# Layer 0's xhat scaling of the last two token blocks placed behind the MoE routing, its buffers in the late room tile

## The chip, the core and the metric

The kernel runs on one core of a Trainium2 chip: TensorE (matmuls), VectorE, ScalarE, GpSimd and SyncE, each with a queue of its own that runs in order, and 16 DMA engines. The metric is the device time of one execution in microseconds; the figure shown for a kernel is the median of its runs.

## The reference, cut to what matters

Two layers over 512 latent tokens and 256 context tokens of width 1024. Each layer is a token mixer, a residual with LayerNorm, a mixture of experts (32 experts in 4 groups, two per token), and a second residual with LayerNorm. Layer 1 handles the 512 latent tokens alone.

```python
x_lat = _layer_norm(DN_ALPHA * x_lat + m_l[2] * y_l, ln_g[layer, 0], ln_b[layer, 0])
f_l = _modulate(x_lat, m_l[3], m_l[4])
...
ffn = _hier_moe(tokens, moe_w_group[layer], moe_b_group[layer], moe_w_router[layer], moe_b_router[layer],
                moe_w1[layer], moe_w3[layer], moe_w2[layer])
x_lat = _layer_norm(DN_ALPHA * x_lat + m_l[5] * ffn[:n_lat].reshape(x_lat.shape), ln_g[layer, 1], ln_b[layer, 1])
```

Two things come out of the first LayerNorm: f, what the experts read, and the residual that is added behind them. The kernel keeps the residual in DRAM as xhat.

## The kernel before, in words

`forward` runs, for each layer, the mixer, `post_mixer`, `moe` and, after layer 0, `post_moe`. A token block is 128 tokens: T = 6 blocks in layer 0 (four latent, two context), T = 4 in layer 1.

`post_mixer` (L1290) projects the mixer's output with the weights `wo` in two column halves. In the second half it takes each block t in turn: the residual sum (L1399 to L1403), the statistics (`ln_stats`, L1266 to L1276), the logits of the router (L1351, L1352) of an earlier block, the transposes that feed them (`turn`, L1339, copied by ScalarE in L1341), and `normalise(t - 1)`. `normalise` (from L1354) does two things with a block x. ScalarE writes xh = (x - mean) / deviation (L1362). In layer 0 GpSimd multiplies xh by ALPHA times the gain `gr` (L1364) and adds ALPHA times the bias `br` (L1365), and ScalarE's queue sends xh to DRAM (`K.xhat`, L1366). Beside it VectorE turns x in place into f, in two steps (L1374, L1375), and ScalarE's queue sends f to DRAM (`K.f`, L1376). In layer 1 the last block's f is made by GpSimd out of xh (L1371, L1372), and xh goes to DRAM unscaled. xh has two buffers in layer 0, in the pool `px`; `gr`, `br` and a small `bt` for the output bias lie in `px` too.

`moe_route` (L759 to L853) then picks the experts, in some forty small VectorE operations on tiles of 128 x 24 to 128 x 192, with two ScalarE exponentials and a few matmuls. `moe_ffn` (L857) handles the experts in 16 pairs. `prep(p)` (from L1014) finds the tokens of a pair: one-hot tiles by VectorE (L875), their matmuls (L889), and an indirect DMA by GpSimd that gathers the rows of f (`load`, L902). Each `prep` leaves a function `second()` that loads the pair's larger count into a GpSimd register (L1036) and, if it is over 64 (L1037), gathers the rest. Before the loop the kernel calls `prep(0)`, `prep(1)` and the two `second()`; inside the loop over 32 experts it calls `prep(p + 2)` for every other expert and its `second()` one expert later. Experts 30 and 31 leave their rows in a tile `room`, 128 x 4096, made at expert 30 in the pool `late`.

The weights come through a ring of buffers: `Stream.pump` has SyncE issue one 2 MB load whenever a buffer is free. Two of the buffers that open behind `post_mixer` are held back on purpose, by a one-element GpSimd copy into the buffer (L190): one copy waits for the last block's f, three more stand behind the first gather.

What sets the order of the work: a planner fixes the order of each engine's queue when the kernel is compiled. It starts from the order of the source and from the dependences; `issue_after` adds such a dependence by hand. What came out is read from the trace.

Of the kernel before, what the change touches and what calls it, by code (L numbers as in the profile page):

```python
# [11 lines left out]
F = mybir.dt.float32  # L12
FR = mybir.dt.float32r
# [3 lines left out]
ALU = mybir.AluOpType  # L17
# [283 lines left out]
def row_bcast(ap, n):  # L301

    return bass.AP(tensor=ap.tensor, offset=ap.offset, ap=[[0, 128], [1, n]])
# [553 lines left out]
def moe_ffn(K, l, T, pos, val, cnt, tok0, Y, weights, pool, fx):  # L857

    nc, c = K.nc, K.cst
    V, S, G, PE = nc.vector, nc.scalar, nc.gpsimd, nc.tensor  # L860
    ps, stream = K.ps, K.stream
# [68 lines left out]
    def after(ins):  # L930
        return K.tc.issue_after(ins) if ins else nullcontext()
# [21 lines left out]
    def turn_h(h, s):  # L953
        a = 64 * s
        q = bank("q")
        for j in range(4):
            last = PE.transpose(q[:, 64 * j:64 * j + 64], h[a:a + 64, j:512:4], c["ident"][a:a + 64, a:a + 64]).ins  # L957
        hT = pool.tile([128, 4, 64], F, tag="hT", name="hT", bufs=2)
        V.tensor_copy(hT, q[:, 0:256].rearrange("p (j m) -> p j m", j=4))  # L959
        return hT, last  # L960
# [85 lines left out]
    for second in seconds:  # L1046
        second()
    seconds.clear()
    rest = nc.values_load(cnt[0:1, 64:65], min_val=0, max_val=T * 128)

    def more_blocks(w1, w3):
# [50 lines left out]
    for n in range(33):  # L1102
        p, s = divmod(n, 2)
        turned = []

        def inner():
            hT, last = turn_h(prev["h"], 1 - s)
            turned.append(hT)
            return last

        if n == ROOM:
            K.room = stream.get(("room", l)) if l else (fx.tile([128, 4096], FR, name="room"), None)
            room = K.room[0]
        if n == POST and l:
            K.posts = [stream.get(("post", l, i)) for i in range(2)]
            with after(late_ins):
                residuals(K)
        if n < 32:
            e = 2 * PAIRS[p] + s
            _, oh2, gate, idx = pairs[p]  # L1120
            slots = [stream.get((k, l, e)) for k in ("w1", "w3")]
            w1, w3 = (t[0] for t in slots)
            rv = nc.values_load(cnt[0:1, e:e + 1], engines=engs, min_val=0, max_val=T * 128)
            h = ffn_in(xT[:, :, 64 * s:64 * s + 64], w1, w3, s, gate[:, 0:1], "h", prev and inner)
            if s == 0:
                prep(p + ahead)
            elif p < 15:
                xT = turn_x(x)
        else:
            inner()  # L1130
        if prev:
            w2 = stream.get(("w2", l, prev["e"]))
            if s:
                y = pool.tile([128, 1024], F, tag="y", name="y", bufs=2)

            def second():
                with K.tc.If(prev["rv"] > 64):
                    more_out(prev["h2"], 1 - s, w2[0], prev["idx"][:, 1:2])

            q = ffn_products(turned[0], w2[0])  # L1140
            if n == 32:

                h2 = hidden("h2")
                with after(K.last_mm):
                    with K.tc.If(rv > 64):
                        second_in(15, 1)
                        more_out(h2, 1, w2[0], idx[:, 1:2])
                more_blocks(w1, w3)
                stream.done(*slots)
                sums(K, l, Y)  # L1150
            rows_out(q, y[64 - 64 * s:128 - 64 * s])
            if s == 0 and p > first_late:
                ins = rows_of(y, p - 1 - first_late)
                if n == 30:
                    late_ins = ins
            elif s == 0:
                put(y, prev["idx"][:, 0:1], slice(0, 128))
            if n < 32:
                second()
                stream.done(w2)  # L1160
            if n == 28:

                z = pool.tile([128, 512], F, tag="xTo", name="zeros")
                i2 = pool.tile([128, 4], I32, name="i2")
                G.memset(z, 0.0)
                for o in range(4 if l else 2):
                    V.tensor_scalar(i2[:, o:o + 1], pairs[first_late + o // 2][3][:, 0:1], 2.0, float(o % 2),
                                    op0=ALU.mult, op1=ALU.add)
                    put(z, i2[:, o:o + 1], slice(0, 128), 2)
        if n < 31:  # L1170
            h2 = hidden("h2")
            with K.tc.If(rv > 64):  # L1172
                second_in(p, s)
            if n == 30:
                tokens_of(pairs[15][0], 1 if l else 0)
            if n == 30 and l:
                tokens_of(slots_of(2 * PAIRS[14], 2, c["iota"], pos, "a", 1), 0)
            stream.done(*slots)
        if s == 0 and p < 15:
            x = xgs[0][(p + 1) % 2]  # L1180
        if s == 1 and seconds:
            seconds.pop()()
        if n < 32:
            prev = dict(e=e, h=h, h2=h2, rv=rv, idx=idx)
# [40 lines left out]
def row(K, pool, key, nm, bufs=1):  # L1225
    t = pool.tile([128, 1024], F, tag=nm, name=nm, bufs=bufs)
    K.nc.sync.dma_start(t, row_bcast(K.rows[key], 1024))
    return t
# [61 lines left out]
def post_mixer(K, l, T, mp, mixp, toks, extra):  # L1290

    nc, c = K.nc, K.cst
    V, S, G, PE = nc.vector, nc.scalar, nc.gpsimd, nc.tensor
    if l:
        K.xe = K.open("xearly", "left")
    px = K.open("px", "left")
    wo = K.open("wo", "right")
    cond = [0] * 4 + [1] * (T - 4)
# [3 lines left out]
    if l:  # L1302
        gb = row(K, px, ("gb", l, 0), "f10")
        ga = row(K, px, ("G1", 0), "f20")
    else:
        bo = wo.tile([33, 1024], FR, name="bo")
        bt = px.tile([128, 1024], F, tag="xh", name="bt", bufs=2)
        ones = wo.tile([33, 128], FR, name="ones")
        S.activation(ones, c["onesf"][0:33], AF.Copy)
        G.memset(bo.bitcast(F), 0.0)  # L1310
        nc.sync.dma_start(bt[0:1], K.a["ebo"])
        S.activation(bo[0:1], bt[0:1], AF.Copy)
        G.tensor_sub(bo[32:33], bt[0:1], bo[0:1].bitcast(F))
# [7 lines left out]
    with K.tc.issue_after(loaded):  # L1321
        gate = [row(K, wo, ("gate", l, i), "gate%d" % i) for i in range(nc_)]
# [1 line left out]
    fTs = {}  # L1324
    f12 = [[row(K, px, ("F%d" % n, l, 0), "f%d0" % n) for n in (1, 2)]]
    if l == 0:
        gr, br = (row(K, px, (n, l), n) for n in ("G0", "B0"))
        for r in (gr, br):
            S.activation(r, r, AF.Copy, scale=ALPHA)
    if l:  # L1330
        K.stream.add(K.xe, 3)
# [22 lines left out]
    def normalise(t):  # L1354

        x = ts[t]
        mu, rs = st[t]
        nm = px.tile([128, 1], F, tag="nm", name="nm", bufs=2)
        V.scalar_tensor_tensor(nm, mu, -1.0, rs, op0=ALU.mult, op1=ALU.mult)

        xh = gate[0] if l and t == T - 2 else px.tile([128, 1024], F, tag="xh", name="xh", bufs=2 - l)
        S.activation(xh, x, AF.Identity, scale=rs, bias=nm)  # L1362
        if l == 0:
            G.tensor_mul(xh, xh, gr)  # L1364
            G.tensor_add(xh, xh, br)  # L1365
        S.dma_start(K.xhat[l][t], xh)  # L1366
        if cond[t] == len(f12):
            f12.append([row(K, px, ("F%d" % n, l, 1), "f%d0" % n) for n in (1, 2)])
        f1, f2 = f12[-1]
        if l and t == T - 1:  # L1370
            G.tensor_mul(x, xh, f1)  # L1371
            G.tensor_add(x, x, f2)  # L1372
        else:
            V.scalar_tensor_tensor(x, x, mu, f1, op0=ALU.subtract, op1=ALU.mult)  # L1374
            V.scalar_tensor_tensor(x, x, rs, f2, op0=ALU.mult, op1=ALU.add)  # L1375
        S.dma_start(K.f[128 * t:128 * t + 128], x)  # L1376

    st = []
# [1 line left out]
    for h in range(2):  # L1380
# [8 lines left out]
        for t in range(T):  # L1389
# [8 lines left out]
            xh = ts[t][:, 512 * h:512 * h + 512]  # L1398
# [30 lines left out]
    r = moe_route(K, T, L, mo, fr)  # L1429
# [5 lines left out]
def moe(K, l, T, pools, pos, val, cnt, tok0):  # L1435

    Y = K.dram.tile([2 * T * 128, 1024], F, name="Y%d" % l)
    mo, xr = pools
    fx = None
    if l == 0:  # L1440
        fx = K.fx = K.open("late", "left")
    ff = K.open("ffn", "left")
    w = [K.a[n][l].rearrange("e (p j) f -> e p (j f)", j=j) for n, j in (("w1", 8), ("w3", 8), ("w2", 4))]
    moe_ffn(K, l, T, pos, val, cnt, tok0, Y, w, ff, fx)
    K.close(mo)
    if l:
        K.left = xr, ff, K.xe
    else:
        K.close(ff)
        K.close(xr)  # L1450
    return Y
# [129 lines left out]
def residuals(K):  # L1581

    xh, (a1, a2, _, _) = [[s[0][:, 1024 * n:1024 * n + 1024] for n in range(4)] for s in K.posts]
    V = K.nc.vector
    for x in xh:
        V.scalar_tensor_tensor(x, x, ALPHA, a1, op0=ALU.mult, op1=ALU.mult)
        V.scalar_tensor_tensor(x, a2, ALPHA, x, op0=ALU.mult, op1=ALU.add)
# [717 lines left out]
```

## Time and profile before

| | |
|---|---|
| runs | 1982.54, 1983.78 and 1989.46 us, median 1983.78 |
| the profiled execution, its own time | 1984.09 us |
| its span, first to last instruction | 1982.3 us |
| TensorE busy | 1723.8 us |
| VectorE busy | 934.8 us |
| GpSimd busy | 495.2 us |
| mean granted TensorE clock | 0.934 |

The profile is one execution; its times are counted from the span's start. Engines are PE (TensorE matmuls), PEld (its weight loads), DVE (VectorE), ACT (ScalarE), POOL (GpSimd) and SP (SyncE); a q behind a name is the engine's sequencer or its DMA queue. L1364 is line 1364 of the kernel. "xh<-xh,G" is an output and its inputs by the program's names. A row of the view in order of time has the start, the duration, the engine, the line, the operation, the tiles and shapes, how many were merged, and in brackets the idle time before it and what ended it. PEclk is the granted clock as a share of 2.4 GHz.

### The profile page before, as it was taken

How to read it: one execution, taken by the hardware profiler on the slowest of the kernel's cores; microseconds unless marked ns; L12 is line 12 of the kernel's file. 1: busy time of each engine (PE TensorE's matmuls, PEld its weight loads, DVE VectorE, ACT ScalarE, POOL GpSimd, SP SyncE). 2: the span in 40 equal slices, each digit the busy share in tenths (PEclk: the TensorE clock that was granted, in tenths of full speed). 3: DMA queues.
4: the chain of work that ended last, by engine and by line, in shares of the span. 5: the costliest groups of instructions: out<-in, count | busy, mean ns of one | idle time of the engine just before them, and what ended most of it. 6: DMA issues, size and time to landing. Idle time of an engine off the chain costs nothing. (4 is left out here: it accounts for less than half of the span.)

```text
span 1982.3 us, 22945 instructions
## 1 busy us (share of the span) xinstructions
PE 1723.8 (87%) x8347; PEld 901.1 (45%) x8355; DVE 934.8 (47%) x1651; ACT 459.0 (23%) x774; POOL 495.2 (25%) x433
## 2 busy tenths in 40 slices
PE   5989999958989999999858878999599999988795
PEld 3668556853333333333336654558433333333232
DVE  4786554782222222221187799676623223222137
ACT  3572342220100100010145453343200000000001
POOL 2153464340101000101045576443101001000103
PEclk8999999968999999999979788899799999999998
DMA  9731314258898999989961114417669999999973
GB/s 368 316 126 43 134 83 157 99 196 318 337 425 358 421 426 402 418 343 386 389 266 43 43 43 170 171 43 311 226 277 425 404 425 395 425 426 425 425 300 148
DMA packets 59022, 551.87 MB, mean 278 GB/s; under 512 B 13295, under 2 KB 13807, under 8 KB 28018
## 3 DMA queue, kind: packets, MB, share of 16 engines
q1 hardware_dynamic: 43490, 514.47, 63.5%
q0 software_dynamic: 11056, 21.00, 2.8%
q10 hardware_dynamic: 4320, 14.33, 1.9%
q8 instruction: 97, 1.59, 0.3%
q14 instruction: 59, 0.48, 0.1%
HBM read 535.02 MB, written 33.61 MB: 287 GB/s over the span
## 5 line engine op out<-in xcount | busy, mean ns | idle before, releaser
L940 PE MATMUL q<-ring,xT 128*64 128x512 f32 x1024 | 479.7, 612 | 44.5 <-PEq L1172 27.0
L941 PE MATMUL q<-ring,xT 128*64 128x512 f32 x1024 | 480.9, 614 | 6.4 <-DMA ring<-in_w_dram 3.5
L969 PE MATMUL q<-ring,hT 128*64 128x512 f32 x1152 | 300.2, 610 | 24.1 <-DMA ring<-in_w_dram 10.2
L940 PEld LDWEIGHTS q<-ring,xT 128*64 128x64 f32 x1024 | 133.4, 140 | 302.0 <-issue 269.6
L949 ACT ACTIVATE sl<-q 64x512 f32<-64x512 f32 x72 | 42.6, 591 | 756.2 <-PE q L941 745.0
L902 POOL DMA_INDIRECT xg<-f,tok x38 | 39.1, 1028 | 595.4 <-DVE tok L897 406.9
L969 PEld LDWEIGHTS q<-ring,hT 128*64 128x64 f32 x1152 | 89.2, 139 | 181.9 <-issue 168.8
L941 PEld LDWEIGHTS q<-ring,xT 128*64 128x64 f32 x1024 | 133.9, 140 | 26.0 <-issue 16.6
L959 DVE COPY hT<-q 128x256 f32<-128x256 f32 x72 | 30.6, 425 | 240.1 <-PE q L957 239.7
L278 PE MATMUL pj<-hh,wlo 128*128 128x512 f32 (+2 forms) x336 | 108.5, 373 | 15.8 <-DVE wlo L267 15.8
L278 PE MATMUL pj<-hl,whi 128*128 128x512 f32 (+2 forms) x336 | 105.9, 364 | 0.0
L278 PE MATMUL pj<-hh,whi 128*128 128x512 f32 (+2 forms) x336 | 105.3, 363 | 0.0
L1839 POOL TENSOR_TENSOR acc<-acc,prod 128x512 f32<-128x512 f32 x56 | 87.4, 1561 | 56.1 <-ACT prod L1838 53.1
L875 DVE TENSOR_TENSOR oh<-cf,pos 128x512 fp32r<-128x512 f32 (+1 forms) x65 | 53.3, 822 | 98.9 <-PE qi L889 97.9
L977 DVE TENSOR_TENSOR y<-q,m 64x512 f32<-64x512 f32 x70 | 48.2, 689 | 81.5 <-PE q L969 74.8
L980 DVE COPY y<-q 64x512 f32<-64x512 f32 x37 | 25.7, 693 | 114.4 <-ACT y L979 76.5
L915 DVE COPY xT<-qx 128x512 f32<-128x512 f32 x32 | 22.1, 692 | 120.9 <-PE qx L911 120.9
L950 DVE SCALAR_TENSOR_TENSOR h<-q,gate,sl 64x512 f32<-64x512 f32 x68 | 51.0, 749 | 56.6 <-ACT sl L949 39.2
L1834 DVE SCALAR_TENSOR_TENSOR acc<-glu,pv,acc 128x512 f32<-128x512 f32 x60 | 73.5, 1230 | 0.9
L278 PEld LDWEIGHTS pj<-hh,wlo 128*128 128x128 f32 (+1 forms) x336 | 59.1, 196 | 31.6 <-DVE wlo L267 15.9
L984 POOL DMA_INDIRECT Y<-y,idx x33 | 32.8, 993 | 147.1 <-DVEq L1172 71.7
L957 PEld LDWEIGHTS q<-cf,h 64*128 64x128 f32 x288 | 39.8, 209 | 59.3 <-issue 55.8
(530 smaller groups left out, 3087.3 us busy)
## 6 DMA issues: line engine op xcount, KB each, us to landing
ring<-in_w_dram SPq DMA_DIRECT2D x192, 2048.0 KB, 18.7
ring<-in_wmod_dram SPq DMA_DIRECT2D x24, 2048.0 KB, 10.6
ring<-Y SPq DMA_DIRECT2D x8, 1024.0 KB, 9.7
ring<-in_ew_dram SPq DMA_DIRECT2D x3, 2048.0 KB
f<-t ACTq DMA_DIRECT2D x10, 512.0 KB, 4.1
xhat<-xh ACTq DMA_DIRECT2D x9, 512.0 KB, 3.8
ring<-in_ewo_dram SPq DMA_DIRECT2D x2, 2048.0 KB, 11.0
ring<-in_ow_dram SPq DMA_DIRECT2D x2, 2048.0 KB, 16.5
```

Of the source, the lines that this page charges most:

```text
L278: nc.tensor.matmul(q[0:m, 0:s1 - s0], a[:, k, 0:m], b[k][:, s0:s1], start=(k == i == 0), stop=(k == 7 and i == 2))
L875: V.tensor_tensor(oh.rearrange("p t (n s) -> p t n s", n=n), iota[:, None, None, :].to_broadcast([128, T, n, 64]), pos[:, :, e:e + n, None ...
L902: return G.indirect_dma_start(out=x[0:m], out_offset=None, in_=K.f, in_offset=bass.IndirectOffsetOnAxis(ap=tok[0:m], axis=0), bounds_check ...
L940: PE.matmul(q[a:a + 64], xT[:, k, :], w1[:, 512 * k:512 * k + 512], start=(k == 0), stop=(k == 7))
L941: last = PE.matmul(q[b:b + 64], xT[:, k, :], w3[:, 512 * k:512 * k + 512], start=(k == 0), stop=(k == 7)).ins
L949: S.activation(sl[a:a + 64], q[a:a + 64], AF.Silu)
L950: V.scalar_tensor_tensor(h[a:a + 64], q[b:b + 64], gate[a:a + 64], sl[a:a + 64], op0=ALU.mult, op1=ALU.mult)
L957: last = PE.transpose(q[:, 64 * j:64 * j + 64], h[a:a + 64, j:512:4], c["ident"][a:a + 64, a:a + 64]).ins
L969: K.last_mm = PE.matmul(q[64 * o:64 * o + 64], hT[:, k, :], w2[:, 1024 * k + 512 * o:1024 * k + 512 * o + 512], start=(k == 0), stop=(k == ...
L977: V.tensor_mul(y[:, b], q[a], K.m5[a, b])
L1834: V.scalar_tensor_tensor(y, g[:, k:k + NL], w(k), y, op0=ALU.mult, op1=ALU.add)
L1839: G.tensor_add(z, z, p)
```

## The change

The scaling of xhat for blocks 4 and 5 of layer 0, and the DMA that stores it, become functions that `moe_ffn` calls on GpSimd behind the two `second()` ahead of the expert loop. So that xh, `gr` and `br` outlive `px`, they move into one tile `spare` in the pool `late`, which is opened before `px` and shares its room with the later `room` tile. In layer 1, the last block's f is made by VectorE as for the other blocks.

```diff
@@ moe_ffn
     seconds.clear()
+    if l == 0:
+        for scaled in K.after:
+            scaled(G)
     rest = nc.values_load(cnt[0:1, 64:65], min_val=0, max_val=T * 128)
@@
         if n == ROOM:
-            K.room = stream.get(("room", l)) if l else (fx.tile([128, 4096], FR, name="room"), None)
+            K.room = stream.get(("room", l)) if l else (fx.tile([128, 4096], FR, tag="room", name="room"), None)
@@ post_mixer
     if l:
         K.xe = K.open("xearly", "left")
+    else:
+
+        K.fx = K.open("late", "left")
+        spare = K.fx.tile([128, 4096], F, tag="room", name="spare")
+        spare = [spare[:, 1024 * n:1024 * n + 1024] for n in range(4)]
+        K.after = []
     px = K.open("px", "left")
@@
-        bt = px.tile([128, 1024], F, tag="xh", name="bt", bufs=2)
+        bt = spare[2]
@@
     if l == 0:
-        gr, br = (row(K, px, (n, l), n) for n in ("G0", "B0"))
-        for r in (gr, br):
+        gr, br = spare[0:2]
+        for r, n in ((gr, "G0"), (br, "B0")):
+            nc.sync.dma_start(r, row_bcast(K.rows[n, l], 1024))
             S.activation(r, r, AF.Copy, scale=ALPHA)
@@ normalise
-        xh = gate[0] if l and t == T - 2 else px.tile([128, 1024], F, tag="xh", name="xh", bufs=2 - l)
+        xh = spare[2 + t % 2] if l == 0 else gate[0] if t == T - 2 else px.tile([128, 1024], F, tag="xh", name="xh")
         S.activation(xh, x, AF.Identity, scale=rs, bias=nm)
-        if l == 0:
-            G.tensor_mul(xh, xh, gr)
-            G.tensor_add(xh, xh, br)
-        S.dma_start(K.xhat[l][t], xh)
+
+        def scaled(E):
+            if l == 0:
+                G.tensor_mul(xh, xh, gr)
+                G.tensor_add(xh, xh, br)
+            E.dma_start(K.xhat[l][t], xh)
+
+        if l == 0 and t > T - 3:
+            K.after.append(scaled)
+        else:
+            scaled(S)
@@
-        if l and t == T - 1:
-            G.tensor_mul(x, xh, f1)
-            G.tensor_add(x, x, f2)
-        else:
-            V.scalar_tensor_tensor(x, x, mu, f1, op0=ALU.subtract, op1=ALU.mult)
-            V.scalar_tensor_tensor(x, x, rs, f2, op0=ALU.mult, op1=ALU.add)
+        V.scalar_tensor_tensor(x, x, mu, f1, op0=ALU.subtract, op1=ALU.mult)
+        V.scalar_tensor_tensor(x, x, rs, f2, op0=ALU.mult, op1=ALU.add)
@@ moe
     if l == 0:
-        fx = K.fx = K.open("late", "left")
+        fx = K.fx
```

## Rows read from the trace of the kernel before

**Rows 1.** The page: busy time, share of the span and instructions of each engine.
```profile
PE 1723.8 (87%) x8347; PEld 901.1 (45%) x8355; DVE 934.8 (47%) x1651; ACT 459.0 (23%) x774; POOL 495.2 (25%) x433
```
**Rows 2.** Windows: us, busy PE, PEld, DVE, ACT, POOL, granted clock, DMA share, GB/s.
```profile
330.00:408.00 78.00, 78.00 (x395) 61.66 (x393) 52.70 (x91) 17.76 (x28) 27.82 (x12) 1.00 0.43 163
410.00:429.00 19.00, 8.24 (x48) 7.65 (x47) 16.23 (x31) 4.62 (x7) 11.36 (x4) 0.62 0.64 243
429.00:442.00 13.00, 3.77 (x25) 3.53 (x24) 10.26 (x50) 5.50 (x7) 0.21 (x1) 0.50 0.66 242
```
**Rows 3.** GpSimd in order of time, 411 to 430 us (layer 0, blocks 4 and 5).
```profile
412.36 2.45 POOL L1364 TENSOR_TENSOR xh<-xh,G 128x1024 f32<-128x1024 f32 x1 [3.47 <-ACT xh L1362]
414.88 3.20 POOL L1365 TENSOR_TENSOR xh<-xh,B 128x1024 f32<-128x1024 f32 x1
422.18 2.35 POOL L1364 TENSOR_TENSOR xh<-xh,G 128x1024 f32<-128x1024 f32 x1 [4.09 <-ACT xh L1362]
424.60 3.37 POOL L1365 TENSOR_TENSOR xh<-xh,B 128x1024 f32<-128x1024 f32 x1
429.19 0.21 POOL L190 COPY ring<-t 1x1 f32<-1x1 f32 x1 [1.23 <-DVE ge L772]
```
**Rows 4.** VectorE in order of time, the same stretch, logits and f steps.
```profile
413.37 2.51 DVE L1374 SCALAR_TENSOR_TENSOR t<-t,mv,f 128x1024 f32<-128x1024 f32 x1
415.81 2.33 DVE L1352 SCALAR_TENSOR_TENSOR L<-L,mv,bi 128x36 f32<-128x36 f32 x1
418.12 1.27 DVE L1375 SCALAR_TENSOR_TENSOR t<-t,mv,f 128x1024 f32<-128x1024 f32 x1
...
419.86 0.26 DVE L1352 SCALAR_TENSOR_TENSOR L<-L,mv,bi 128x36 f32<-128x36 f32 x1
...
423.27 1.30 DVE L1352 SCALAR_TENSOR_TENSOR L<-L,mv,bi 128x36 f32<-128x36 f32 x1
424.50 1.27 DVE L1374 SCALAR_TENSOR_TENSOR t<-t,mv,f 128x1024 f32<-128x1024 f32 x1
...
425.80 3.24 DVE L1375 SCALAR_TENSOR_TENSOR t<-t,mv,f 128x1024 f32<-128x1024 f32 x1
```
**Rows 5.** Lines 1036 (430 to 445 us) and 1037 (to 455): ns, first and last start.
```profile
L1036 POOLq TENSOR_LOAD <-cnt x8: 283/290/492, 439.2 to 444.6; - x8
...
L1037 POOLq COMPARE_BRANCH  x3: 38/40/55, 445.2 to 448.0; - x3
```
**Rows 6.** ScalarE in order of time: DMA issues of xhat and f.
```profile
418.33 0.33 ACTq L1366 DMA_DIRECT2D xhat<-xh  x1
...
419.42 0.85 ACTq L1376 DMA_DIRECT2D f<-t  x1
```
**Rows 7.** GpSimd in order of time, 440 to 470 us: the gathers.
```profile
442.40 1.75 POOL L902 DMA_INDIRECT xg<-f,first  x1 [12.99 <-PE qi L889]
...
466.00 0.99 POOL L902 DMA_INDIRECT xg<-f,tok  x1 [14.40 <-DVE tok L897]
```
**Rows 8.** VectorE and GpSimd in order of time, layer 1's routing.
```profile
1411.96 0.19 DVE L773 TENSOR_TENSOR ae<-ae,cf 128x32 f32<-128x32 f32 x1
...
1412.11 2.34 POOL L1371 TENSOR_TENSOR t<-xh,f 128x1024 f32<-128x1024 f32 x1 [41.25 <-ACT xh L1362]
...
1412.41 2.09 DVE L777 TENSOR_TENSOR ao<-ae,ai 128x32 f32<-128x32 f32 x1
1414.53 2.40 POOL L1372 TENSOR_TENSOR t<-t,f 128x1024 f32<-128x1024 f32 x1
...
1414.64 2.43 DVE L799 TENSOR_TENSOR A<-go,ao 128x128 f32<-128x128 f32 x1
...
1418.21 0.28 DVE L799 TENSOR_TENSOR A<-go,bo 128x128 f32<-128x128 f32 x1
```
**Rows 9.** VectorE and TensorE in order of time: h of the first expert.
```profile
462.21 0.75 DVE L950 SCALAR_TENSOR_TENSOR h<-q,gate,sl 64x512 f32<-64x512 f32 x1
...
467.80 0.45 PE L957 MATMUL q<-cf,h 64*128 64x64 f32 x2
```

## The prediction

> **What bounds the kernel now.** I read the page first, then stretches, then engines in order of time. TensorE is busy for 87% of the span [rows 1], so work of GpSimd can only count where TensorE stands still. The view by windows finds that place [rows 2]. From 330 to 408 us TensorE is busy in all 78.00 us: while the output projection of layer 0 runs, nothing that VectorE or GpSimd does late is seen. From 410 to 429 us it works 8.24 of 19.00 us, from 429 to 442 us 3.77 of 13.00, and VectorE works 16.23 and 10.26. So from 410 us on the end is set by VectorE's chain: statistics, logits and f of the last two token blocks (4 and 5 of 0 to 5; the change's "last rows"), then the routing, then the first gather.
>
> Now the two engines side by side. GpSimd's four operations on blocks 4 and 5 take 2.45, 3.20, 2.35 and 3.37 us [rows 3]. VectorE's instructions are long exactly inside them [rows 4]: L1352 takes 0.26 us where GpSimd is idle, but 2.33 us from 415.81, ending at 418.14, just after GpSimd's multiply and add end at 418.08; L1374 takes 1.27 us free and 2.51 us beside GpSimd; L1375 takes 1.27 us free and 3.24 us when begun at 425.80 under GpSimd's add. The late ones finish about as long after GpSimd's end as they take alone: they wait, they don't share. Together the four long ones cost (2.51-1.27)+(2.33-0.26)+(1.30-0.26)+(3.24-1.27) = 6.3 us of the chain. That is the prize if GpSimd's four operations leave this place.
>
> **Part 1: does the move take place?** The source puts the four operations behind the gathers of the first pairs, but each engine's order is fixed when the program is compiled, and an instruction that depends on nothing later may be put earlier. The trace shows how far. `second()` loads a count into a GpSimd register (L1036) and branches on it (L1037). At the place where the change inserts its calls the source has issued two such loads; the other 14 of layer 0 are issued one by one inside the expert loop, behind branches on the same queue. Yet eight of them were done before 445 us, ahead of the first branch at 445.2 [rows 5]. What was ready went ahead of branches and gathers before it in the source. The moved operations need only xh, gr and br, and GpSimd stood idle for 3.47 and 4.09 us before the two multiplies until ScalarE had written xh [rows 3], and nothing in `scaled` ties them to a gather. So I expect all four to stay where they are, at 412 to 428 us, and the 6.3 us of waiting with them. Change: 0; bounds 0 and -6.3.
>
> **Part 2: xhat of blocks 4 and 5 leaves by GpSimd's queue.** Two issues leave ScalarE's queue. The one at 418.33 is followed by f's issue, which takes 0.85 us against 0.33 for the one before it [rows 6]; the second fT copy stands behind it on ScalarE and feeds the last logits, for which VectorE waits. Without xhat in front I give f 0.33 us: -0.5 us; bounds 0 and -0.85. On GpSimd no plain DMA is seen; the nearest are the gathers, 0.99 to 1.75 us each [rows 7]. Block 4's issue falls into the 4.09 us of idle time, block 5's behind the add that ends at 427.97, ahead of the copy that frees a ring slot, due at 429.19 [rows 3]. It can push that copy by 427.97+1.75-429.19 = 0.5 us; the copy lets a weight load of the second expert go, and the first expert's h is only at 462.21 [rows 9]. Cost 0, at most +0.5.
> The Trainium skill speaks against this queue: "SBUF — State Buffer", section "Summary: rules for kernel authors", has the descriptors of a DMA issued by GpSimd starved while VectorE runs in its fast modes, and would issue it from ScalarE's or SyncE's queue; by the rows the sum is 1982.0, by that page it would be that of rival D.
>
> **Part 3: buffers.** gr, br and xh keep their sizes but lie in the later room tile, so the other tiles of px move. Loads may be issued a little sooner or later, and the room tile waits for these readers before expert 30. The loads' time is covered by the 78 us in which TensorE does not stop; were that cover gone, a late row would show as a stall before 408 us. Cost 0.
>
> **Part 4: layer 1, f of the last block.** GpSimd's L1371 and L1372, 2.34 and 2.40 us, go; VectorE's L1374 and L1375 come, 2 x 1.27 = 2.5 us by the free rows [rows 4, 8]. In their shadow the routing lost (2.09-0.19)+(2.43-0.28) = 4.05 us, with L773 at 0.19 and the second L799 at 0.28 as the free rows [rows 8]. Net -4.05+2.5 = -1.5 us if they stand where xh is ready: GpSimd, which waited for it, began at 1412.11. f overwrites the tile that xh is read from, so if the compiled order puts L1374 earlier, the routing behind it on VectorE waits too. I allow one short step of misplacement, 0.2 us (L773's length), and take -1.3, near the -1.5 because f becomes ready with xh in either kernel; the bounds are -4.05 (f wholly in VectorE's gaps) and +1.1 (2.6 us of waiting, as if L1374 stood ahead of the first routing step).
>
> **Sum.** The profiled execution took 1984.09 us. -0.5 -1.3 = -1.8 gives 1982.3; the median shown, 1983.78, is 0.3 below that execution, so 1982.0. Earlier routing carries on into the experts because the next weight loads wait for TensorE and for copies behind the first gather, which move with it.
>
> **Rivals.**
> A, the forecast: the four operations stay. Their bounds give 1979 to 1985.
> B, the move happens as said. For it: the calls stand behind the gathers in the source, and a compiler that weighs them last may keep them there. Against it: rows 5. GpSimd is idle for 14.40 us ahead of the gather at 466.00 [rows 7]; the four operations (11.4 us) and two issues (2.0 to 3.5) about fill it. VectorE's h at 462.21 may end up to 3.4 us late, but TensorE wants it at 467.80 [rows 9], a margin of 467.80-462.96 = 4.8 us. So all 6.3 us come in: 1982.0-6.3 = 1975.7.
> C, slower: the four operations fall between, into 429 to 442 us, where GpSimd has 0.21 us of work and VectorE runs the routing [rows 2]. A two-input operation there then waits as L777 and L799 do in layer 1; 11.4 us on, less the 6.3 saved, is +5.1: 1987.1. It decides if the multiplies begin after 425 us and before the first gather. For it: a free engine. Against it: their inputs are ready at 412 and 422 us.
> D, the new issue holds up GpSimd: block 5's xhat issue, due at 427.97, gets no turn while VectorE works through the routing, and ends only just ahead of the first gather at 442.40 [rows 7], which then comes later by one such issue and the copy of L190 behind it, 1.75 + 0.21 us [rows 3, 7]: 1984.0, no change. Against it: the gather at 442.40 itself went out beside VectorE's work, in 1.75 us.
>
> **How the numbers follow.** A 0.66, B 0.22, C 0.08, D 0.04. The likeliest gives 1982.0. The range has to reach B (1975.7, with 1.7 below for its own small terms) and C's 1987.1 with 0.9 above: 1974 to 1988; A's own is 1979 to 1985. About 0.5%, 9.9 us, is what a measurement of this kernel tells from no change. No case reaches it by its terms: even B is -8.1 us. I leave 0.12 for faster (B with a further gain where TensorE's granted clock, 0.50 (1.2 of 2.4 GHz) in the routing, where it is idle for most of the time [rows 2], rises sooner), 0.04 for slower (C with a stalled gather behind GpSimd's work), and 0.84 for the same.
>
> **What would show it.** Part 1 is right if GpSimd's multiplies of blocks 4 and 5 still begin near 412 and 422 us and the f step beside them is still over 3 us; if they begin after 445 us and VectorE's logits and f steps are 0.26 and 1.27 us, B is right. Part 2: f's issue near 419 us at 0.33 us, and two new xhat issues on GpSimd's queue. Part 4: no GpSimd work between 1409 and 1417 us, L777 and L799 under 0.3 us, and f's first step beginning within 0.3 us of the end of xh. A stall of TensorE before 408 us, or a first expert whose h is late, would prove my zero terms wrong.

## The result and the profile after

The changed kernel took 1968.89 us (median of 9 runs, 1958.56 to 1976.16), the kernel before 1982.54 us in the same job: 13.7 us between the medians. The ratio on record is 0.9938, interval 0.9910 to 0.9966, which makes it 12.3 us or 0.6% faster. The forecast was 1982.0 us, range 1974 to 1988, "the same": the time lies below the range. The profiled execution of the changed kernel has a span of 1969.8 us, 12.5 less than before.

The page's busy row answers to [rows 1]. No engine has notably less to do than before (GpSimd 6.7 us less, TensorE 2.8 more), so the gain is idle time of TensorE.

```profile
PE 1726.6 (88%) x8347; PEld 908.5 (46%) x8355; DVE 936.7 (48%) x1653; ACT 458.5 (23%) x774; POOL 488.5 (25%) x433
```

**Layer 0.** GpSimd in order of time answers to [rows 3], VectorE's long steps to [rows 4], f's issue to [rows 6], the first gather to [rows 7]. Lines moved: L1376, L1377 are the old L1364, L1365; L1362, L1387, L1388 the old L1352, L1374, L1375; L1378 and L1389 issue xhat and f.

```profile
418.96 2.44 POOL L1376 TENSOR_TENSOR spare<-spare 128x1024 f32<-128x1024 f32 x1 [3.47 <-ACT spare L1372]
421.48 3.21 POOL L1377 TENSOR_TENSOR spare<-spare 128x1024 f32<-128x1024 f32 x1
425.01 0.78 POOL L1378 DMA_DIRECT2D xhat<-spare  x1 [0.32 <-POOL spare L1377]
428.54 2.33 POOL L1376 TENSOR_TENSOR spare<-spare 128x1024 f32<-128x1024 f32 x1 [2.76 <-ACT spare L1372]
430.95 3.37 POOL L1377 TENSOR_TENSOR spare<-spare 128x1024 f32<-128x1024 f32 x1
435.56 0.20 POOL L190 COPY ring<-t 1x1 f32<-1x1 f32 x1 [1.24 <-DVE ge L772]
436.01 0.61 POOL L1378 DMA_DIRECT2D xhat<-spare  x1 [0.26 <-POOL ring L190]
448.35 1.08 POOL L902 DMA_INDIRECT xg<-f,first  x1 [11.73 <-DVE val L844]
...
419.97 2.51 DVE L1387 SCALAR_TENSOR_TENSOR t<-t,mv,f 128x1024 f32<-128x1024 f32 x1
422.41 2.34 DVE L1362 SCALAR_TENSOR_TENSOR L<-L,mv,bi 128x36 f32<-128x36 f32 x1
429.54 1.39 DVE L1362 SCALAR_TENSOR_TENSOR L<-L,mv,bi 128x36 f32<-128x36 f32 x1
432.16 3.25 DVE L1388 SCALAR_TENSOR_TENSOR t<-t,mv,f 128x1024 f32<-128x1024 f32 x1
...
426.03 0.33 ACTq L1389 DMA_DIRECT2D f<-t  x1
```

The four operations did not move: they stand before the routing, and the four VectorE steps are as long as before. The stretch lies 6 to 7 us later in this execution. Executions without the layer 0 parts have that too (block 4's xh starts 8.1 us later in e1 and 7.1 in e5 below), so it does not belong to the change.

**Layer 1.** VectorE in order of time answers to [rows 8]: f's two steps stand in the chain, L777 and L799 are short.

```profile
1412.77 0.19 DVE L773 TENSOR_TENSOR ae<-ae,cf 128x32 f32<-128x32 f32 x1
1412.88 1.28 DVE L1387 SCALAR_TENSOR_TENSOR t<-t,mv,f 128x1024 f32<-128x1024 f32 x1
...
1414.20 1.28 DVE L1388 SCALAR_TENSOR_TENSOR t<-t,mv,f 128x1024 f32<-128x1024 f32 x1
1415.40 0.18 DVE L777 TENSOR_TENSOR ao<-ae,ai 128x32 f32<-128x32 f32 x1
...
1415.72 0.28 DVE L799 TENSOR_TENSOR A<-go,ao 128x128 f32<-128x128 f32 x1
```

What followed is where the time came from. First the kernel before in order of time: VectorE's first slots, the copy, SyncE's weight load and its register load (by line), the first gather, its landing (by tile), TensorE's first matmuls on slots (qt) and on gathered rows (qx). These rows were there before the prediction, and it did not use them.

```profile
1410.80 1.24 ACT L1362 ACTIVATE xh<-t,nm,mv 128x1024 f32<-128x1024 f32 x1 [0.33 <-DMA xhat<-xh]
1416.99 0.18 POOL L190 COPY ring<-t 1x1 f32<-1x1 f32 x1
...
L1049 SPq TENSOR_LOAD <-cnt x1: 284/284/284, 1420.3 to 1420.3; - x1
...
1420.99 0.34 SPq L194 DMA_DIRECT2D ring<-in_w_dram  x1
...
1421.01 0.40 DVE L844 TENSOR_TENSOR val<-gt,val 128x128 fp32r<-128x128 f32 x1
1421.32 1.28 DVE L875 TENSOR_TENSOR oh<-cf,pos 128x512 fp32r<-128x512 f32 x2
1423.56 0.98 PE L1020 MATMUL qt<-tok,oh 128*128 128x2 f32 x4 [4.13 <-DVE oh L875]
1427.02 1.35 POOL L902 DMA_INDIRECT xg<-f,first  x1 [9.85 <-DVE info L892]
DMA to landing us min/median/max: 8.0/8.0/8.0
1435.11 1.94 PE L911 MATMUL qx<-cf,xg 128*128 128x128 f32 x8 [6.68 <-DMA xg<-f,first]
```

Then the same of the changed kernel:

```profile
1411.18 1.23 ACT L1372 ACTIVATE xh<-t,nm,mv 128x1024 f32<-128x1024 f32 x1
1415.61 0.24 POOL L190 COPY ring<-t 1x1 f32<-1x1 f32 x1 [43.68 <-DVE ao L777]
1415.88 0.33 SPq L194 DMA_DIRECT2D ring<-in_w_dram  x1
1418.73 1.27 DVE L875 TENSOR_TENSOR oh<-cf,pos 128x512 fp32r<-128x512 f32 x2
1419.55 0.98 PE L1020 MATMUL qt<-tok,oh 128*128 128x2 f32 x4 [1.17 <-DVE oh L875]
...
L1052 SPq TENSOR_LOAD <-cnt x1: 288/288/288, 1420.3 to 1420.3; - x1
...
1421.03 0.39 DVE L844 TENSOR_TENSOR val<-gt,val 128x128 fp32r<-128x128 f32 x1
...
1423.39 1.13 POOL L902 DMA_INDIRECT xg<-f,first  x1 [7.54 <-issue]
DMA to landing us min/median/max: 3.6/3.6/3.6
1427.21 1.94 PE L911 MATMUL qx<-cf,xg 128*128 128x128 f32 x8 [1.22 <-DMA xg<-f,first]
```

Counted from the last xh, the first gather goes out 4.0 us earlier (12.2 for 16.2) and lands in 3.6 us instead of 8.0: qx 16.0 for 24.3. Two things changed order. On SyncE the weight load now stands ahead of the register load of the routing's count; before, it waited behind it from the copy at 1416.99 to 1420.99. On VectorE the first slots (L875) stand ahead of the last gate value (L844). Nobody wrote either order down; with f on another engine the compiled order came out differently.

### The profile page after: what moved, and what is told of

It is laid out like the page before. It is cut to its first block, busy times and chain, and to the rows that moved or that the text cites. A ratio compares the mean times of both kernels' runs of the same rounds, so it can differ in the third digit from the quotient of the medians.

```text
span 1969.8 us, 22935 instructions
## 1 busy us (share of the span) xinstructions
PE 1726.6 (88%) x8347; PEld 908.5 (46%) x8355; DVE 936.7 (48%) x1653; ACT 458.5 (23%) x774; POOL 488.5 (25%) x433
## 5 line engine op out<-in xcount | busy, mean ns | idle before, releaser
L949 ACT ACTIVATE sl<-q 64x512 f32<-64x512 f32 x72 | 42.5, 591 | 750.4 <-PE q L941 740.0
L1852 POOL TENSOR_TENSOR acc<-acc,prod 128x512 f32<-128x512 f32 x56 | 85.7, 1532 | 57.3 <-ACT prod L1851 54.4
L875 DVE TENSOR_TENSOR oh<-cf,pos 128x512 fp32r<-128x512 f32 (+1 forms) x65 | 53.3, 822 | 97.5 <-PE qi L889 96.4
L984 POOL DMA_INDIRECT Y<-y,idx x33 | 32.7, 992 | 147.9 <-DVE y L980 70.8
L940 PE MATMUL q<-ring,xTo 128*64 128x512 f32 x128 | 61.4, 637 | 7.7 <-DVE xTo L924 7.7
## 6 DMA issues: line engine op xcount, KB each, us to landing
ring<-in_w_dram SPq DMA_DIRECT2D x192, 2048.0 KB, 17.7
ring<-Y SPq DMA_DIRECT2D x8, 1024.0 KB, 10.7
```

The lines of the kernel that those rows point to most:

```text
L875: V.tensor_tensor(oh.rearrange("p t (n s) -> p t n s", n=n), iota[:, None, None, :].to_broadcast([128, T, n, 64]), pos[:, :, e:e + n, None ...
L940: PE.matmul(q[a:a + 64], xT[:, k, :], w1[:, 512 * k:512 * k + 512], start=(k == 0), stop=(k == 7))
L949: S.activation(sl[a:a + 64], q[a:a + 64], AF.Silu)
L984: st = G.indirect_dma_start(out=Y.rearrange("r (n d) -> (r n) d", n=n), out_offset=bass.IndirectOffsetOnAxis(ap=idx[r], axis=0), in_=y[r], ...
L1852: G.tensor_add(z, z, p)
```

## The experiments

All measures below are taken inside one profile, from the start of an xh on ScalarE. **Layer 0, h:** from the xh of block 4 to the transposes of the first expert's h (L957). **Layer 1:** from the last xh to the issue of the first gather, its landing, qx, and the transposes of h. The account is the sum of both h differences to the kernel before.

| kernel | layer 0 h | gather | landing | qx | layer 1 h | account | ratio, interval |
|---|---|---|---|---|---|---|---|
| before | 56.8 | 16.2 | 8.0 | 24.3 | 42.9 | | |
| changed | 53.4 | 12.2 | 3.6 | 16.0 | 33.3 | -13.1 | 0.9938, 0.9910 to 0.9966 |
| e1 | 57.3 | 12.2 | 3.4 | 16.0 | 33.4 | -9.1 | 0.9953, 0.9933 to 0.9973 |
| e2 | 53.4 | 16.5 | 7.8 | 24.5 | 43.2 | -3.0 | 0.9971, 0.9949 to 0.9992 |
| e3 | 53.3 | 13.9 | 3.6 | 17.7 | 34.3 | -12.1 | 0.9921, 0.9891 to 0.9951 |
| e4 | 53.4 | 12.1 | 10.6 | 22.8 | 42.5 | -3.7 | 0.9967, 0.9948 to 0.9987 |
| e5 | 57.4 | 16.9 | 3.6 | 20.6 | 39.3 | -3.0 | 0.9997, 0.9976 to 1.0018 |
| e6 | 56.5 | 11.8 | 3.4 | 15.5 | 32.7 | -10.5 | 0.9929, 0.9904 to 0.9953 |
| e7 | 49.7 | 12.2 | 3.4 | 16.0 | 33.4 | -16.6 | 0.9894, 0.9861 to 0.9928 |
| e11 (changed) | 53.5 | 12.0 | 3.4 | 15.7 | 33.2 | -13.0 | 0.9927, 0.9905 to 0.9949 |
| e12 (as e7) | 49.6 | 11.9 | 3.3 | 15.7 | 33.1 | -17.0 | 0.9921, 0.9897 to 0.9944 |
| e13 | 56.4 | 16.2 | 9.3 | 25.6 | 43.4 | +0.1 | 1.0000, 0.9974 to 1.0025 |

Each account, as a share of 1982 us, lies inside the interval of its own kernel (the changed kernel's 13.1 us is 0.66%, for 0.62% measured). So the two stretches hold the whole effect, as far as these intervals, 4 to 7 us to either side, can tell. The rest of the span is 1882.6 us in the kernel before and 1883.2 in the changed one; in the other profiles of the table it lies between 1876.4 and 1884.8 us. Profiles with the same order and the same rows differ by under 1 us in layer 1: with the order of before, h comes at 42.9, 43.2 (e2) and 43.4 us (e13); with the changed order at 32.7 to 33.4.

**e1: Part 4 alone.** To the kernel before:

```diff
-        if l and t == T - 1:
-            G.tensor_mul(x, xh, f1)
-            G.tensor_add(x, x, f2)
-        else:
-            V.scalar_tensor_tensor(x, x, mu, f1, ...)
-            V.scalar_tensor_tensor(x, x, rs, f2, ...)
+        V.scalar_tensor_tensor(x, x, mu, f1, ...)
+        V.scalar_tensor_tensor(x, x, rs, f2, ...)
```

> The kernel before, with Part 4 alone: f of the last block of layer 1 on VectorE, everything in layer 0 as before. Measured in layer 1 from the start of the last xh on ScalarE: the first matmul on gathered rows (qx) came 24.3 us later in the kernel before and 16.0 us later in the changed one; the transposes of the first expert's h 42.9 and 33.3 us. Theory 1 (the gain is Part 4, and most of it comes from what its new order does behind it: first slots earlier on VectorE, the weight load ahead of SyncE's register load): qx at 16.0 +- 1, h at 33.3 +- 1.5, whole kernel 0.4 to 0.7% faster. Rival (the gain is in the layer 0 parts or the buffers): qx falls by only the 1.1 us that the locks gave, and the time is within 0.2% of before.

Measured: qx at 16.0, h at 33.4, ratio 0.9953: theory 1. The edit of six lines, without the buffers and the moved calls, brings the new orders and three quarters of the gain.

**e2: the layer 0 parts alone** (the changed kernel with the lines above put back).

> The changed kernel with Part 4 undone: f of layer 1's last block on GpSimd again, layer 0 parts and buffers as changed. Theory 1: layer 1 as in the kernel before (qx 24.3 us, h 42.9 us behind the last xh), whole kernel within 0.3% of before (layer 0's routing to first expert is 3 us shorter in the changed kernel, its part before the routing 6 us longer). Rival: 0.4 to 0.7% faster, as the changed kernel. It also shows whether the 3 us by which TensorE's work between 355 and 362 us came later (granted clock 0.78 against 1.00) belong to the change: if they do, they are here too.

Layer 1 is as before. The time is 0.29% lower, interval 0.08 to 0.51%: at the edge of theory 1, which had named the 3 us but held them to be taken up by the later start of the stretch before. So the layer 0 parts gain too, 3.3 us in layer 0's stretch. The lower granted clock behind 355 us (0.78 over 355 to 365 us) is here as well, but also in e1 and e5, which have no layer 0 part: it does not belong to the change.

**e5 and e4: the weight load and the gather.** e5, to the kernel before:

```diff
+    K.loaded = K.stream.last
...
-    rest = nc.values_load(cnt[0:1, 64:65], ...)
+    with K.tc.issue_after(K.loaded):
+        rest = nc.values_load(cnt[0:1, 64:65], ...)
```

> The kernel before with one tie added: in layer 1 SyncE's register load of the largest count stands behind the weight load that the copy of L190 lets go, so that the load goes out at about 1417.2 instead of 1421.0 us. Nothing else moves. Theory (the first gather lands late because this 2 MB load is still moving when the gather is issued at 1427.0): it lands in about 4 us instead of 8.0, qx comes 20 to 21 us behind the last xh instead of 24.3, the time is 0.2% shorter. Rival (the gather is slow for another reason, its own late issue or f's write in front of it): 8 us again, no change of time.

e4, to the changed kernel, moves the call that lets the load go behind the routing, in layer 1:

```diff
-    K.stream.add(xr, 1, end, ts[T - 1][0:1, 0:1], total=extra)
+    if l == 0:
+        K.stream.add(xr, 1, end, ts[T - 1][0:1, 0:1], total=extra)
...
+    if l:
+        K.stream.add(xr, 1, end, r[2][0:1, 64:65], total=extra)
```

> The changed kernel, with the weight load of layer 1 that a copy of L190 lets go bound to the counts of the routing instead of to f, so that it leaves about 9.7 us behind the last xh (in the kernel before 10.2, in the changed one 4.7). VectorE's order stays as changed. Theory (a 2 MB load in flight makes the first gather land late): landing 7.5 to 10 us instead of 3.6, qx at 20 to 22 us instead of 16.0, h at 37 to 39 instead of 33.3. Rival (the landing follows the gather's own issue time, not the load): landing under 4.5 us, qx within 1 us of 16.0. Whole time about 4 us above the changed kernel's by the theory.

In e5 the gather landed in 3.6 us and qx came at 20.6, both as the theory said; the row m5 (0.5 MB) also left later there, 16.1 us behind the last xh against 10.7, so e5 alone does not say which transfer was in the way. Here h came 3.6 us earlier, of the 9.7 us that it gained in the changed kernel. Its account of 3.0 us is too small for its interval; the whole time shows nothing. e4 moves the 2 MB load alone. SyncE, GpSimd, the landing and TensorE in e4:

```profile
1417.01 0.33 SPq L870 DMA_DIRECT2D m<-row_m  x1
1419.44 4.34 SPq L194 DMA_DIRECT2D ring<-in_w_dram  x2
...
1422.10 1.12 POOL L902 DMA_INDIRECT xg<-f,first  x1 [2.68 <-issue]
DMA to landing us min/median/max: 10.6/10.6/10.6
1432.78 1.94 PE L911 MATMUL qx<-cf,xg 128*128 128x128 f32 x8 [8.19 <-DMA xg<-f,first]
```

The gather went out as early as in the changed kernel and landed in 10.6 us instead of 3.6; qx came at 22.8 and h at 42.5, where the kernel before has 42.9. Landing, qx and h all lie past the theory's ranges, on its side. So nearly the whole gain of layer 1 is lost without the early load, and e5 shows that the early load does not bring it alone: it takes the load out of the way and the gather sent early. Where it leaves late, sending the gather 4.1 us earlier brings qx only 1.5 us (24.3 to 22.8), because qx comes 13.3 us behind the load (1432.78-1419.44) and 14.1 us in the kernel before (1435.11-1420.99).

**e3: the order on VectorE.** To the changed kernel, with K.valued the last gate value (L844):

```diff
-            oh = slots_of(e, 2, c["iota"], pos, "a", 1)
+            with after(K.valued if l and p == 0 else None):
+                oh = slots_of(e, 2, c["iota"], pos, "a", 1)
```

> The changed kernel, with the order of the kernel before given back at one place: in layer 1 the slots of the first pair (oh, L875) may only be issued on VectorE behind the gate values (L844). SyncE's order, with the weight load in front, stays as changed. Theory (the changed order on VectorE is a term of its own, near 3 us): from the last xh of layer 1, qt comes at 11.0 to 11.5 us instead of 8.4, the first gather is issued at 14.5 to 15 instead of 12.2, still lands in 3.4 to 4 us, qx at 18 to 18.8 instead of 16.0, h at 35.5 to 36 instead of 33.3. Rival (the slots are not what the first gather waits for; the locks and the load's order make the whole difference): qx stays within 0.7 us of 16.0. The whole time would be 2.6 us longer than the changed kernel's, too little to be told by itself.

The gather went out at 13.9, qx at 17.7, h at 34.3: the order on VectorE is a term of 1.7 us at the gather and 1.0 at h, half of what I had expected. In this one profile it is the smaller of the two.

**e8: the price of the four operations.** The changed kernel without GpSimd's scale and bias of blocks 4 and 5, whose rows go out unscaled. Layer 1 then gets other rows, so only layer 0 is read; the whole time (ratio 1.0021) is no measure of the edit.

```diff
-            if l == 0:
+            if l == 0 and t <= T - 3:
                 G.tensor_mul(xh, xh, gr)
```

> The changed kernel without GpSimd's multiply and add of blocks 4 and 5 in layer 0: the scale and bias of the residual rows of these two blocks are left out, their rows go out unscaled. This is the price of the four operations where they stand. Theory (they cost VectorE's waits, part of which TensorE and ScalarE hide, as the run with the tie showed by a gather 4.2 us earlier): from the xh of the next to last block, the first gather at 26 to 27 us (changed kernel 30.7), qx at 31 (35.2), h at 49 (53.4); 4 us faster than the changed kernel. The prediction's own price, 6.3 us, would give 24.4, 28.9 and 47.1.

From the xh of block 4: the gather at 25.8, qx at 30.1, h at 48.4, for 30.7, 35.2 and 53.4 in the changed kernel. The four operations cost 5.0 us where they stand; rival B's 6.3 us was right but for 1.3.

**e6, e7, e12: the move made to happen.** e6 ties the calls behind the first gather, e7 and e12 behind that of the second pair. The edit of e7 and e12, to the changed kernel (e6 takes `K.gathered` from the first gather's `load`):

```diff
-                load(xgs[0][p % 2], tok[:, 0:1], 128)
+                gathered = load(xgs[0][p % 2], tok[:, 0:1], 128).ins
+                if p == 1:
+                    K.gathered = gathered
...
-        for scaled in K.after:
-            scaled(G)
+        with K.tc.issue_after(K.gathered):
+            for scaled in K.after:
+                scaled(G)
```

> The changed kernel with GpSimd's four operations and two issues of layer 0 really tied behind the first gather. Theory (rival B of the prediction): the four long VectorE steps take 1.27 and 0.26 us, the routing and the first gather of layer 0 come some 6 us earlier against the end of the output projection, the late operations fill GpSimd's idle time in the first expert; 0.3% faster than the changed kernel, 0.9% faster than before. Rival: the operations now wait against VectorE's work in the first expert (xT copies, h) and give most of it back; as the changed kernel within 0.1%.

> The changed kernel with GpSimd's four operations and two issues of layer 0 tied behind the gather of the second pair, past VectorE's slots of that pair, on which they fell when tied behind the first gather (one slots instruction took 8.59 us there). Theory: all of the earlier routing comes in: from the xh of the next to last block of layer 0, qx at 31 us (changed kernel 35.2, tied behind the first gather 37.2), h at 49 to 50 (53.4 and 56.5); 4 us faster than the changed kernel, 0.8% faster than before. Rival: the operations hold up VectorE's slots and h of the first expert's end, and h comes at 51 to 53; 1 to 2 us faster than the changed kernel.

In e6 the four VectorE steps took 1.25, 0.25, 0.26 and 1.28 us (2.51, 2.34, 1.39 and 3.25 in the changed kernel), so it was GpSimd's operations that had held them. The gather went out 4.2 us earlier, and yet h came 3.1 us later than in the changed kernel: the rival's case, in this stretch. GpSimd, VectorE and TensorE in e6:

```profile
442.75 1.24 POOL L902 DMA_INDIRECT xg<-f,first  x1 [12.60 <-DVE val L844]
...
444.40 4.63 POOL L1379 TENSOR_TENSOR spare<-spare 128x1024 f32<-128x1024 f32 x2
448.99 2.33 POOL L1380 TENSOR_TENSOR spare<-spare 128x1024 f32<-128x1024 f32 x1
...
443.55 8.59 DVE L875 TENSOR_TENSOR oh<-cf,pos 128x768 fp32r<-128x768 f32 x1 [1.60 <-PE qi L889]
...
452.19 1.44 PE L889 MATMUL qi<-val,oh 128*128 128x8 f32 x6 [7.40 <-DVE oh L875]
```

One VectorE instruction that takes 0.96 us by itself took 8.59: it ended 0.8 us after GpSimd's third operation in a row (451.32), and TensorE stood 7.40 us for it. The Trainium skill, "SBUF — State Buffer", section "SBUF: two separate sides", has VectorE and GpSimd share a port that the first of them holds for one whole instruction; the waiting agrees, but here it lasted over three of GpSimd's instructions, and VectorE's instruction is recorded as begun before the first of them (443.55 and 444.40). In e7 the operations ran from 453.35 to 462.6 us, in the gap named in the prediction, and one slots instruction took 3.50 us without anybody waiting for it: h at 49.7, the theory's number. The whole time was 1963.24 us, 0.9894 of before. To compare it with the changed kernel on one chip:

> The changed kernel itself, once more, for a comparison on the same chip with the kernel that ties the four operations behind the second pair's gather. By the account (3.4 us in layer 0, 9.7 us in layer 1): 13.1 us, 0.66% faster than before; rival (the first measurement was partly chance): under 0.4%.

> The changed kernel with the four operations and two issues tied behind the gather of the second pair, as before. By the account of local times (7.1 us in layer 0, 9.6 us in layer 1): 16.7 us, 0.84% faster than the kernel before, 3.6 us (0.18%) faster than the changed kernel on the same chip. Rival (its first result, 1.06%, is whole): 8 us faster than the changed kernel.

e11, the changed kernel, came to 0.9927 (0.73% for the expected 0.66%), and e12 to 0.9921, medians 1967.58 and 1966.26 us. The 4.0 us at the first expert are there again (53.5 and 49.6), but the whole times cannot be told apart, which the expected 3.6 us also allow. Both beat the kernel before; that e7's order beats the changed kernel is not shown.

**e10 and e13: why layer 0 gained.** Behind the first gather the layer 0 parts changed the place of 12 small matmuls (qi, L889) on TensorE. Before, all 12 stand between the first two experts; in the changed kernel 8 stand there. e10 and e13 put them inside the first expert, to the kernel before. The edit of e13:

```diff
-            h = ffn_in(..., prev and inner)
+            first = l == 0 and n == 0
+            h = ffn_in(..., (lambda: prep(ahead)) if first else prev and inner)
             if s == 0:
-                prep(p + ahead)
+                if not first:
+                    prep(p + ahead)
```

> The kernel before, with the slots and values of the third pair (12 small matmuls qi, L889) issued inside the first expert of layer 0, behind its fourth step, instead of between the first and the second expert. In every kernel so far with the order of before, these 12 stand between the two experts and the next 3 to 4 pairs of TensorE steps take 1.06 us each; in every one with the layer 0 parts of the change some of them stand inside the first expert and no step of the second is over 0.64 us. Theory (the place of these small matmuls is what the layer 0 parts gained): no step of 1.06 us in the second expert, from the first matmul of the first expert to the transposes of its h 15.2 to 15.6 us (with the 12 inside it) instead of 16.7; the whole 0.1% faster than before, within its interval. Rival (the slow steps come from the longer stop of TensorE before the second expert, whatever stands there): 1.06 us steps again, 16.5 us or more.

e10 also turned another tile of x in front of the second expert, which then works on other rows; it is read up to there only. No step of its second expert took over 0.64 us, but that turning filled the stop. e13 is the same without it:

> The kernel before, with the 12 small matmuls qi (L889) of the third pair issued inside the first expert of layer 0 and the second pair's x turned where it is turned before. So TensorE's queue has nothing between the first expert's last step and the second expert's first. Theory (the place of these small matmuls is what the layer 0 parts gained behind the first gather): the stop between the two experts is 1.0 to 1.6 us, no step of the second expert takes over 0.7 us, and from the first matmul of the first expert to the transposes of its h it is 15.0 to 15.6 us instead of 16.7. Rival (the slow steps follow any stop of this length): three to four pairs at 1.06 us in the second expert, 16.7 us or more. Whole time: 0.1% below before by the theory, within its interval either way.

The second expert's first step in the kernel before, and in e13:

```profile
462.59 1.09 PE L940 MATMUL q<-ring,xT 128*64 128x512 f32 x1 [0.74 <-PEq L1172]
```
```profile
467.45 0.61 PE L940 MATMUL q<-ring,xT 128*64 128x512 f32 x1 [1.74 <-PEq L1174]
```

The slow steps run at a granted clock of 0.50 (1.2 GHz; 462.6 to 465.2 us before), the steps of e13 at 1.00 (2.4 GHz; 467.5 to 470.9 us). They are gone although TensorE's idle time in front is longer. From the last step of the first expert to the first of the second it is shorter, though, 1.7 us for 2.2; but e6 has 2.3 us there, eight of these matmuls and no slow step, so the length alone does not make them. In layer 0, the three profiles with 11 or more of these matmuls between the two experts (before, e1, e5) have the slow steps and the other eleven do not. But the stop, 1.7 us for the theory's 1.0 to 1.6, takes most of it back: 16.3 us from the first expert's first matmul to h, outside the theory's 15.0 to 15.6, for 16.7 before, and 15.3 in the changed kernel. So the place of these matmuls is shown to remove the slow steps; that it makes the changed kernel's gain is shown for 0.4 us only.

## Why the prediction was wrong

**Part 1** held: all four operations stayed, with their waits. The place named for rival B was right too: made to happen there (e7), the move brings 3.7 us at the first expert's h, not 6.3.

**Part 2** held by its instruction: f's issue took 0.33 us, the two xhat issues on GpSimd 0.78 and 0.61, one of them even behind the copy; the first gather's issue took 1.08 us, so rival D did not occur: no run here shows the starved queue of the Trainium skill's "SBUF — State Buffer", section "Summary: rules for kernel authors". Block 5's xhat landed 9.5 us behind its issue on GpSimd's queue, and on ScalarE's queue 4.1 us (e1) and 10.1 us (e13) behind it, so the landing does not show it either. By e2's stretch of layer 0 the layer 0 parts brought 3.3 us, where the sum had 0.5. Between the xh of block 4 and h the changed kernel gained 0.3 up to the last xh (f's issue, as predicted), 0.4 up to the gather, 0.6 from there to qx (5.1 to 4.5 us; the gather's own instruction took 1.08 us for 1.75), 0.6 from qx to the first expert and 1.5 inside it. All but the first stand behind orders that came out differently and that the prediction took as fixed; which of them makes which part is open, but for the 0.4 us of e13.

**Part 3**: no stall before 408 us comes with the change; e2 and e1 bear the zero out.

**Part 4** was right for what it priced. The routing's matmul pps came 8.02 us after the last xh before and 6.58 in the changed kernel: -1.4 for the predicted -1.3. (f's first step began 0.47 us behind the end of xh, not within 0.3.) **The step that failed is the sentence below the sum: that an earlier routing carries on unchanged because the next weight loads "move with it".** They did not move with it. The load that counts waits neither for TensorE nor for a copy behind the gather: it is let go by the copy that waits for f, and in the kernel before it then stood 4.0 us behind SyncE's register load. It left 5.5 us earlier against the last xh (4.7 for 10.2), far more than the routing's 1.4, and the gather 4.0. TensorE's first rows came 8.3 us earlier, h 9.7. The runs put the difference on the load being out of the gather's way (e4: 9.3 of the 9.7 us at h are lost if it leaves late; e5: 3.6 come with the early load alone) and on the slots' place on VectorE (e3: 1.0). They overlap and do not add up. Of the 9.7 us, 1.4 come behind qx (17.2 us to h for 18.6): the second expert's first steps have a granted clock of 0.51 in the kernel before (1448.9 to 1452.2 us) and of 1.00 in the changed one (1440.9 to 1444.3 us). e13, with the order of before in layer 1, has 1.00 there too, so this part is not tied to the change.

The chances followed: no case held a gain of more than 8.1 us, since each rival was about the operations that the change speaks of, and none about the compiled order of what it does not touch. The prediction had used that very order, in [rows 5], to say that the calls would not stay where they were written, and then held all other orders fixed.

## What to carry to other kernels

Where a compiler fixes each engine's order, moving an operation to another engine can reorder queues that the edit does not name; price such a change by a range that has room for a reordered queue next to a wait, above all a DMA queue on which a large load stands behind a register load. Before a small latency-bound gather, look at what else is in flight when it is issued: its landing time, not its issue, may be the term. Calls moved in the source are not moved in the program unless a dependence or a tie holds them, and once tied, they want a gap in the work of the engine that waits for them.

## What the hardware showed unexpectedly

A gather of 0.5 MB landed in 3.3 to 3.6 us where the 2 MB load before it had left 7.5 us or more earlier, in 7.8 to 9.3 us where it had left 6.0 us earlier (before, e2, e13), and in 10.6 us where it had left 2.7 us earlier (e4). Not every profile keeps to this: in e8, whose layer 1 has other rows, it landed in 5.5 us, 7.5 us behind the load. VectorE waited over three GpSimd instructions in a row, not one (8.59 us, e6). And the granted clock of one stretch differs from profile to profile, between kernels that are written alike up to there: from 355 to 365 us, in the projection of layer 0, the windows of the kernel before, e1, e5 and e13 (granted clock third from the end) show

```profile
355.00:365.00 10.00, 10.00 (x76) 9.31 (x75) 3.77 (x8) 1.21 (x1) 0.32 (x1) 1.00 0.58 208
```
```profile
355.00:365.00 10.00, 10.00 (x48) 8.38 (x47) 4.61 (x8) 2.23 (x3) 1.36 (x1) 0.68 0.49 169
```
```profile
355.00:365.00 10.00, 10.00 (x52) 8.46 (x51) 6.21 (x9) 5.13 (x8) 2.77 (x2) 0.82 0.20 48
```
```profile
355.00:365.00 10.00, 10.00 (x60) 8.36 (x59) 5.89 (x9) 4.81 (x8) 2.76 (x2) 1.00 0.23 54
```

with TensorE busy in all 10 us each time. 0.68 and 0.82 are means over parts at 1.00 and parts at 0.50 (from 360 to 365 us in e1 it is 0.50). The windows do not hold quite the same matmuls, 48 to 76 of them. What lowers the clock in some profiles is not settled here; whole times spread by 1% (1970.85 to 1992.39 us for the kernel before in one job), which is why the account was taken from stretches.
